# Two pools of weight buffers placed above the split activations in the on-chip memory

## The chip, the cores and the metric

The kernel runs on one core of one Trainium2 chip. The metric is the device time of one execution in microseconds (us), as the median of several runs; lower is better. Before the change it is 3458.62 us (three runs, 3456.98 to 3459.93).

## The reference

The reference computes two transformer-like blocks in float32 over 1024 tokens of 1024 features. The first block mixes the tokens by a gated linear attention in two directions (four heads) that starts from a context of 256 tokens, and by a gated spatial mix; the second by a recurrence with a short convolution and by attention inside a window of 128 tokens. Each block ends with a gated feed-forward layer of 2816 hidden features. Between them lie norms over the features. What costs time are the products of the activations with the weight matrices:

```python
x = x + g1 * mix_l
x = x + g2 * _swiglu(_modulate(_rmsnorm(x, norm2_g[l]), sh2, sc2), w_ffn_in[l], w_ffn_out[l])
...
proj = xn @ w_in[l]
...
x = x + merged @ w_out[l]
gu = xn2 @ w_ffn_in[l]
x = x + (jax.nn.silu(ff_gate) * ff_up) @ w_ffn_out[l]
```

## The kernel before, in words

Activations lie with 128 features on the partitions and the tokens along the row, in tiles of 128 by 512. To reach float32 accuracy each operand of a large product is held as two parts in the matrix format float32r, a high part and a low part, and each product is three matmuls: high weights by high activations, high weights by low activations, low weights by high activations. In `gemm` (lines 158 to 167) and in `product` of `ffn_in` and `ffn_out` (lines 1051 to 1053 and 1264 to 1266) the weights are the stationary operand, loaded anew for each matmul, 128 columns at a time, and the activations stream past them, nearly always 512 columns. In `gemm_tok` (lines 169 to 177) it is the other way round: a block of 128 tokens of the activations is stationary and the weights stream, 256 columns.

Weights come from memory into `raw` (2 buffers of 4 KB in each partition), and are split by `unit` (lines 139 to 152): ScalarE writes the high part `wh`, GpSimd (POOL) the low part `wl`, both in the pool `wp` (4 buffers of 4 KB of each name). The two feed-forward layers split quarters and sums of weights straight into `wp` by `split` (lines 190 to 193). SyncE issues the loads in the order of the program. Tiles that hold split activations for long come from the pool `hp` (32 buffers `hl` of 2 KB); others come from the pools of a phase, `slot` or `half`, which lie behind all of these. In the last of five blocks of each second feed-forward product the weights are kept: `supply` (lines 1202 to 1214) hands `unit` two buffers `hl` in which to put the two parts, so that the stationary operand comes from `hp` there and the streaming one from `half`. It does so in pieces of 512 columns in the first layer, and in pieces of 512 and 256 columns in the second.

The pools that live for the whole program are opened in `__init__` (lines 59 to 69), and each pool lies in a partition right behind the one opened before it. Their sizes follow from their tiles, in bytes of a partition: `raw` 8,192; `wp` 32,768; `tmp` (4 tiles `t` of 2 KB) 8,192; `sm` (small tiles: five names of 4 by 32 bytes, one of 4 by 64, five single ones of 64) 1,216; `hp` 65,536. In the compiled program of before `raw` starts at byte 20,992, which is 164 times 128, so `wp` starts at 29,184, `tmp` at 61,952, `sm` at 70,144, and `hp` at 71,360; the pools of the phases start at 136,896.

No order is written out by hand around the change: it touches no instruction, and every loop, queue and buffer count stays.

Of the kernel before, what the change touches and what calls it, by code (L numbers as in the profile page):

```python
# [16 lines left out]
P = 128  # L17
T = 1024
# [31 lines left out]
def hs(q):  # L50
    """The columns of half q of the tokens."""
    return slice(q * HQ, q * HQ + HQ)


class Prog:
    """Activations lie feature-major, [features on partitions, tokens], in tiles of 128
    features by 512 tokens; operands of the large products as exact sums of two float32r parts."""

    def __init__(self, tc, ins, out, ctx):
        self.tc, self.nc, self.I, self.out = tc, tc.nc, ins, out  # L60
        self.cst = self.pool(ctx, "cst", 1)
        self.raw = self.pool(ctx, "raw", 2)
        self.wp = self.pool(ctx, "wp", 4)
        self.tmp = self.pool(ctx, "tmp", 4)
        self.sm = self.pool(ctx, "sm", 4)
        self.hp = self.pool(ctx, "hp", 32)
        self.dr = self.pool(ctx, "dr", 1, space=bass.MemoryType.DRAM)
        self.bg, self.lag, self.loads = deque(), deque(), 0

# [28 lines left out]
    def slot(self, *dims, dt=F32):  # L98
        """[P, 1024] of the phase's storage, or less of it in the shape dims."""
# [8 lines left out]
    def half(self, dt=F32):  # L108
        """[P, 512] of the phase's storage."""
        return self.gp.tile([P, HQ], dt, name="half")  # L110
# [4 lines left out]
    def hnew(self, n=8):  # L115
        """A split activation, hi and lo, each n tiles of features by halves of tokens."""
# [22 lines left out]
    def unit(self, src, kt=8, width=P, eng=None, raw=None, into=None):  # L139
        """Load one block of weights (if it isn't in raw yet) and split it exactly into two float32r parts."""  # L140
# [13 lines left out]
    def wide(self, src, eng=None, raws=(None, None)):  # L154
        """Two blocks, 1024 x 256 together."""
        return [self.unit(src[i], kt=4, width=256, eng=eng if i else None, raw=raws[i]) for i in range(2)]

    def gemm(self, o, w, h, l, q, kt=8, s=slice(None), mid=None):
        """o[feature, token] = W^T X with both operands split; mid comes half way."""
# [9 lines left out]
    def gemm_tok(self, o, ws, h, l, t):  # L169
        """o[token, feature] = X W for the 128 tokens of block t."""  # L170
# [8 lines left out]
    def proj(self, src, fn, mid=None):  # L179
        """The products of one block of weights with both halves of the tokens."""  # L180
# [15 lines left out]
    def tick(self, n=1):  # L196
        """The next step of what runs beside the large products."""
# [14 lines left out]
    def store(self, dst, src):  # L212
        """A store that later loads need not wait behind."""
# [7 lines left out]
    def step(self, chunks, n=1):  # L221
        """One product after the other, with n steps of what runs beside them after each."""
# [5 lines left out]
    def square_into(self, acc, src, first, scale=1.0, eng=None):  # L228
        """acc += (scale * src)^2"""
# [6 lines left out]
    def squares(self, acc, src, eng):  # L236
        """The sum of the squares of tiles."""
# [4 lines left out]
    def token_sums(self, accs, ps, o):  # L242
        """ps[:, o + b] = sums over features for the tokens of block b."""
# [6 lines left out]
    def rsqrt(self, x):  # L250
        """1/sqrt of a small positive tile, by Newton's steps from the exponent's half."""
# [12 lines left out]
    def spread(self, r):  # L264
        """r holds a value for each token, tokens on partitions in blocks: the same on all
        partitions, tokens along the free axis."""
# [6 lines left out]
    def rstd(self, accs, n=D):  # L273
        """1/sqrt(mean of the squares + eps) in a bank, from sums of squares, in two steps."""
# [10 lines left out]
    def now(self, steps):  # L285
        """All steps at once."""
# [6 lines left out]
    def modulated(self, x, rs, A, B, hi, lo, eng=None):  # L293
        """hi + lo = x * A * rs + B"""
# [10 lines left out]
    def norm(self, q, acc, A, B=None):  # L305
        """Steps to the modulated norm of half q of self.x, in the form that ffn_in takes: with quarters Bij
        (i: half of the features, j: of the tokens), B11, B21, B22 and the sums T1..T4, all split."""
# [54 lines left out]
    def ada_first(self):  # L362
        """Shift and scale of the first norm, for the latents and the context, one half of the features after
        the other, by products; most of the scale by sums of weighted rows over k first. In steps."""
# [45 lines left out]
    def ada_one(self, m):  # L410
        """A block of gate 1, shift 2, scale 2, gate 2 of the latents; its sums over k and those of the
        block before over the partitions."""
# [19 lines left out]
    def ada_last(self):  # L432
# [5 lines left out]
        # the branches are summed twice as large  # L438
# [3 lines left out]
    def start(self):  # L442
# [5 lines left out]
        # resets of the scans at the chunks' first tokens  # L448
# [56 lines left out]
    def start_latents(self):  # L505
        """Steps to the norm of the latents."""
# [15 lines left out]
    def decays(self, st, n, zs, d):  # L522
        """Cumulated log decays (times GATE_TEMP) of direction d within each chunk, in steps.
        st: stacked low-rank inputs [96, n]; gives tiles that hold [P, NH, n] in order."""
# [29 lines left out]
    def low_rank(self, waf, st, h, l, n, q):  # L554
        """Inputs of the decays, stacked [hi; lo; hi]."""
# [23 lines left out]
    def latent_decays(self, stl, zs):  # L579
        """Decays of the latents, kept outside."""  # L580
# [36 lines left out]
    def context_states(self, st, zs):  # L617
        """Steps to the states that the context leaves, for both directions."""
        nc = self.nc
        self.Si = self.slots_of(2, NH, 256)  # L620
        for d in QS:
# [7 lines left out]
            # the half that is passed first decays through the other one too  # L629
# [17 lines left out]
    def ends(self, c, d):  # L647
        """Of chunked log decays: the chunks' totals, their exponentials, those of pairs."""
# [1218 lines left out]
```

## Time and profile before

| what | value |
|---|---|
| median of three runs | 3458.62 us (3456.98 to 3459.93) |
| span of the profiled execution, first to last instruction | 3453.9 us |
| what lies around the span, by the runs shown | 3.1 to 6.0 us |
| TensorE matmul busy | 3305.8 us, 96% |
| TensorE weight load busy | 2683.4 us, 78% |
| VectorE (DVE), ScalarE (ACT), GpSimd (POOL) busy | 61%, 39%, 45% |
| DMA | 97 GB/s over the span |

The profiled execution has no time of its own beside its span; the runs' times are a few microseconds longer, since they hold what comes before the first and after the last instruction. Matmuls run through a pipeline: the recorded duration of one (some 390 ns for 512 columns) is longer than the distance between the starts of two that follow each other, and that distance is what a stream of them costs.

### The profile page before, as it was taken

The page shows a single profiled execution, that of the slowest core. Times are in us where ns is not written, and L with a number is a line of the kernel's source. Part 1 is how long each engine was busy: PE and PEld are TensorE (multiplying, and loading weights), DVE is VectorE, ACT ScalarE, POOL GpSimd, SP SyncE. Part 2 cuts the span into 40 slices and gives each one's busy share as a digit, 9 for nine tenths or more (in the row PEclk, how much of TensorE's full clock was granted, in tenths as well). Part 3 has the DMA queues.
Part 4 walks back from the last instruction along what each step waited for, and adds up shares of the span by engine and source line. Part 5 has one row for each costly group of instructions (what it writes and reads, how often), then busy time and mean ns, then how long its engine had stood idle before and what let it go on. Part 6 is the DMA issues. An engine that isn't in the chain of part 4 may idle for free. (4 is left out here: it accounts for less than half of the span.)

```text
span 3453.9 us, 43238 instructions
## 1 busy us (share of the span) xinstructions
PE 3305.8 (96%) x15868; PEld 2683.4 (78%) x15868; DVE 2118.4 (61%) x3438; ACT 1364.3 (39%) x2396; POOL 1544.3 (45%) x991
## 2 busy tenths in 40 slices
PE   7999999999999999999999989999999999999997
PEld 4778888888888778888767867777777778887766
DVE  7554234333667385555698587777776585554786
ACT  4552222211122442232424486666665332232433
POOL 3222233222322675444656434444444775444764
PEclk9999999999999999999999999999999999999999
DMA  6121111244236522221352311111114432222342
GB/s 254 62 110 53 49 68 65 74 159 129 84 119 204 169 92 80 74 82 67 113 177 83 130 33 54 45 54 45 54 48 154 144 103 99 74 80 89 95 137 78
DMA packets 153012, 335.11 MB, mean 97 GB/s; under 512 B 20864, under 2 KB 29184, under 8 KB 152800
## 3 DMA queue, kind: packets, MB, share of 16 engines
q1 hardware_dynamic: 140640, 311.36, 26.8%
q10 hardware_dynamic: 12160, 20.98, 1.6%
q8 instruction: 126, 2.06, 0.2%
q14 instruction: 86, 0.70, 0.1%
HBM read 263.07 MB, written 69.21 MB: 96 GB/s over the span
## 5 line engine op out<-in xcount | busy, mean ns | idle before, releaser
L151 POOL TENSOR_TENSOR wl<-raw,wh 128x1024 fp32r<-128x1024 f32 (+1 forms) x188 | 426.7, 2273 | 751.2 <-ACT wh L150 629.9
L163 PE MATMUL mm<-hl,wh 128*128 128x512 f32 (+1 forms) x1584 | 643.3, 406 | 1.4 <-ACT t L1547 1.4
L165 PE MATMUL mm<-hl,wl 128*128 128x512 f32 (+1 forms) x1584 | 630.7, 398 | 1.6 <-POOL wl L151 1.6
L164 PE MATMUL mm<-hl,wh 128*128 128x512 f32 (+1 forms) x1584 | 631.7, 399 | 0.0
L193 POOL TENSOR_TENSOR wl<-half,wh 128x512 fp32r<-128x512 f32 x308 | 433.0, 1430 | 367.5 <-ACT wh L192 367.5
L150 ACT CAST wh<-raw 128x1024 fp32r<-128x1024 f32 (+3 forms) x189 | 177.4, 940 | 492.3 <-PE mm L164 232.4
L165 PEld LDWEIGHTS mm<-hl,wl 128*128 128x128 f32 (+1 forms) x1584 | 300.5, 190 | 74.6 <-POOL wl L151 2.4
L163 PEld LDWEIGHTS mm<-hl,wh 128*128 128x128 f32 (+1 forms) x1584 | 300.2, 190 | 66.6 <-ACT t L1547 1.8
L164 PEld LDWEIGHTS mm<-hl,wh 128*128 128x128 f32 (+1 forms) x1584 | 300.5, 190 | 64.9 <-issue 0.5
L192 ACT CAST wh<-half 128x512 fp32r<-128x512 f32 x308 | 178.6, 619 | 409.6 <-PE ax L1052 218.1
L1030 DVE TENSOR_TENSOR half<-half 128x512 f32<-128x512 f32 x176 | 202.1, 1188 | 3.0
L1606 POOL TENSOR_SCALAR p<-p,ast 128x384 f32<-128x384 f32 (+1 forms) x64 | 84.0, 1313 | 263.4 <-DVE ast L1604 162.5
L175 PE MATMUL mm<-wh,hl 128*128 128x256 f32 x576 | 163.5, 284 | 1.3 <-ACT wh L150 1.3
L177 PE MATMUL mm<-wl,hl 128*128 128x256 f32 x576 | 161.8, 281 | 1.9 <-POOL wl L151 1.9
L176 PE MATMUL mm<-wh,hl 128*128 128x256 f32 x576 | 162.2, 282 | 0.7 <-DVE hl L193 0.5
L1052 PE MATMUL mm<-hl,wh 128*128 128x512 f32 x360 | 142.8, 397 | 3.3 <-POOL hl L193 3.3
L1051 PE MATMUL mm<-hl,wh 128*128 128x512 f32 x360 | 142.6, 396 | 0.6 <-ACT hl L192 0.6
L1053 PE MATMUL mm<-hl,wl 128*128 128x512 f32 x360 | 142.4, 395 | 0.0
L1051 PE MATMUL ax<-hl,wh 128*128 128x512 f32 x344 | 136.5, 397 | 0.8 <-ACT hl L192 0.7
L1053 PE MATMUL ax<-hl,wl 128*128 128x512 f32 x344 | 136.2, 396 | 0.0
L1052 PE MATMUL ax<-hl,wh 128*128 128x512 f32 x344 | 136.0, 395 | 0.0
L193 POOL TENSOR_TENSOR wl<-raw,wh 128x384 fp32r<-128x384 f32 x96 | 113.8, 1204 | 37.1 <-ACT wh L192 37.1
(419 smaller groups left out, 7991.7 us busy)
## 6 DMA issues: line engine op xcount, KB each, us to landing
half<-in_w_fi SPq DMA_DIRECT2D x196, 256.0 KB, 4.7
hid<-t SPq DMA_DIRECT2D x78, 256.0 KB, 2.0
half<-hid SPq DMA_DIRECT2D x72, 256.0 KB, 4.5
raw<-in_w_ada SPq DMA_DIRECT2D x32, 512.0 KB, 3.7
raw<-in_w_o SPq DMA_DIRECT2D x32, 512.0 KB, 3.9
raw<-in_w_fo SPq DMA_DIRECT2D x32, 384.0 KB, 3.2
slot<-in_w_ada SPq DMA_DIRECT2D x16, 512.0 KB, 10.2
raw<-in_w_u SPq DMA_DIRECT2D x16, 512.0 KB, 3.6
```

The costliest lines, as they stand in the source:

```text
L150: nc.scalar.copy(hi, r)
L151: self.last_split = (eng or nc.gpsimd).tensor_tensor(lo, r, hi.bitcast(F32), op=ALU.subtract).ins
L163: mm(o, wh[:, k], h[k][q][:, s], start=k == 0, stop=False)
L164: mm(o, wh[:, k], l[k][q][:, s], start=False, stop=False)
L165: mm(o, wl[:, k], h[k][q][:, s], start=False, stop=k == kt - 1)
L175: mm(o, h[k][q][:, s], wh[:, k % 4], start=k == 0, stop=False)
L192: self.nc.scalar.copy(hi, x)
L193: (eng or self.nc.vector).tensor_tensor(lo, x, hi.bitcast(F32), op=ALU.subtract)
L1030: V.tensor_tensor(s, a, b, op=op)
L1051: mm(o, wh[:, k], h, start=k == 0, stop=False)
L1052: mm(o, wh[:, k], l, start=False, stop=False)
L1053: mm(o, wl[:, k], h, start=False, stop=k == 3)
```

## The change

The pools `raw` and `wp` are opened after `hp`, no longer before `tmp`. The remainder of the diff empties comments and docstrings, line for line, so that line numbers stay.

```diff
         self.cst = self.pool(ctx, "cst", 1)
-        self.raw = self.pool(ctx, "raw", 2)
-        self.wp = self.pool(ctx, "wp", 4)
         self.tmp = self.pool(ctx, "tmp", 4)
         self.sm = self.pool(ctx, "sm", 4)
         self.hp = self.pool(ctx, "hp", 32)
+        self.raw = self.pool(ctx, "raw", 2)
+        self.wp = self.pool(ctx, "wp", 4)
         self.dr = self.pool(ctx, "dr", 1, space=bass.MemoryType.DRAM)
```

## Rows read from the trace of the kernel before

**Rows 1.** The page: busy us, share of the span and instructions of each engine.
```profile
PE 3305.8 (96%) x15868; PEld 2683.4 (78%) x15868; DVE 2118.4 (61%) x3438; ACT 1364.3 (39%) x2396; POOL 1544.3 (45%) x991
```

**Rows 2.** Waits of PE, longest first: us in total, times, longest.
```profile
PE po L1630 <- DVE pt L193: 20.0, 7, 5.2
PE sc L1595 <- DVE pt L193: 11.0, 12, 1.7
```

**Rows 3.** Busy us (x instructions) of PE, PEld, DVE, ACT, POOL; clock, DMA share, GB/s.
```profile
1650.00:1850.00 200.00, 183.79 (x747) 142.34 (x746) 170.29 (x213) 77.42 (x152) 126.88 (x96) 0.97 0.41 133
1950.00:2650.00 700.00, 654.22 (x3109) 527.45 (x3109) 520.14 (x1057) 467.64 (x890) 289.41 (x161) 0.98 0.17 55
```

**Rows 4.** Timeline of PE, 2900 to 2945: start, duration; first and last of 194 matmuls.
```profile
2899.78 0.39 PE L1051 MATMUL mm<-hl,wh 128*128 128x512 f32 x1
...
2944.81 0.40 PE L1052 MATMUL mm<-hl,wh 128*128 128x512 f32 x1
```

**Rows 5.** Timeline of PE, 1861 to 1886.2: first and last of 113 matmuls.
```profile
1860.62 0.39 PE L164 MATMUL mm<-half,hl 128*128 128x512 f32 x1
...
1886.00 0.39 PE L165 MATMUL ax<-half,hl 128*128 128x512 f32 x1
```

**Rows 6.** The columns of rows 3, for three short stretches.
```profile
1861.00:1886.00 25.00, 25.00 (x112) 20.68 (x111) 16.11 (x24) 14.90 (x24) 7.24 (x6) 1.00 0.26 82
2900.00:2945.00 45.00, 45.00 (x194) 36.28 (x193) 27.28 (x31) 12.18 (x23) 21.99 (x16) 1.00 0.20 71
720.00:760.00 40.00, 40.00 (x176) 32.20 (x175) 9.71 (x24) 2.59 (x3) 4.78 (x2) 1.00 0.39 131
```

**Rows 7.** Timeline of PE, 725 to 743.5: first and last of 81 matmuls.
```profile
724.79 0.39 PE L164 MATMUL mm<-slot,wh 128*128 128x512 f32 x1
...
743.46 0.39 PE L163 MATMUL mm<-slot,wh 128*128 128x512 f32 x1
```

**Rows 8.** Matmuls of line 163: count, duration min/median/max in ns, first and last start.
```profile
L163 PE MATMUL mm<-hl,wh x1584: 387/394/799, 100.9 to 2736.3; 128*128 128x512 f32 x196, 128*96 128x512 f32 x2
...
L163 PE MATMUL mm<-slot,wh x168: 276/394/482, 40.6 to 812.0; 128*128 128x512 f32 x128, 128*128 128x256 f32 x32, 128*96 128x256 f32 x8
...
L163 PE MATMUL ax<-half,hl x80: 283/389/389, 1861.7 to 3438.4; 128*128 128x512 f32 x48, 128*128 128x256 f32 x32
```

**Rows 9.** PE and PEld of one line, whole span: lines 163, 1051, 1264, 175, in this order.
```profile
0.00:3454.00 3454.00, 915.54 (x2296) 434.45 (x2296) 0.99 0.29 97
...
0.00:3454.00 3454.00, 487.84 (x1232) 231.61 (x1232) 0.99 0.29 97
...
0.00:3454.00 3454.00, 137.25 (x336) 65.08 (x336) 0.99 0.29 97
...
0.00:3454.00 3454.00, 183.27 (x640) 123.41 (x640) 0.99 0.29 97
```

**Rows 10.** Timeline of PE, 301 to 306: first and last of 45 matmuls.
```profile
300.90 0.28 PE L177 MATMUL mm<-wl,hl 128*128 128x256 f32 x1
...
306.08 0.28 PE L176 MATMUL mm<-wh,hl 128*128 128x256 f32 x1
```

**Rows 11.** Timeline of PE, 3416.6 to 3418.9: first and last of 22 matmuls.
```profile
3416.33 0.28 PE L164 MATMUL ax<-half,hl 128*128 128x256 f32 x1
...
3418.85 0.28 PE L164 MATMUL mm<-half,hl 128*128 128x256 f32 x1
```

**Rows 12.** PE and PEld of line 163 alone, 1950 to 2650.
```profile
1950.00:2650.00 700.00, 296.28 (x717) 137.47 (x718) 0.98 0.17 55
```

**Rows 13.** Low parts split on POOL by line 193: count, duration min/median/max in ns.
```profile
L193 POOL TENSOR_TENSOR wl<-half,wh x308: 1277/1304/1847, 1193.3 to 3158.6; 128x512 fp32r<-128x512 f32 x154
...
L193 POOL TENSOR_TENSOR half<-half x32: 1276/1592/1840, 1240.2 to 3364.4; 128x512 fp32r<-128x512 f32 x32
```

**Rows 14.** DMA issues: KB each, median us from issue to landing.
```profile
raw<-in_w_u SPq DMA_DIRECT2D x16, 512.0 KB, 3.6
...
slot<-decay SPq DMA_DIRECT2D x8, 512.0 KB, 4.5
```

## The prediction, made before the changed kernel was run

> **What bounds the kernel now.** I read the page first: matmuls keep TensorE (PE) busy for 3305.8 of 3453.9 us, 96%; no other engine is above 61% [rows 1]. The list of PE's waits says the same: the two longest are 20.0 and 11.0 us in total, both behind VectorE in the windowed attention [rows 2]. By stretch, the mixers of the second block leave PE idle for 45.8 of 700 us and the second product of the first feed-forward layer for 16.2 of 200 [rows 3]; in the first product of such a layer it is busy for 45.00 of 45 us [rows 6]. So a change of where buffers lie can matter in two ways: through a transfer or a split that PE waits for, or through what a matmul itself costs.
>
> For the second I read timelines, since the recorded duration of a matmul overlaps its neighbours. In the feed-forward stretch at 2900 us, 194 matmuls of 512 columns without a wait start over 2899.78 to 2944.81: 45.03 / 193 = 233.3 ns each [rows 4]. At 1861 us, 113 of the same shape start over 1860.62 to 1886.00: 25.38 / 112 = 226.6 ns [rows 5]. The granted clock is 1.00, the 2.4 GHz level, in both [rows 6]. What differs is where the stationary operand lies: in `wh` and `wl` in the first, in `hl` in the second, the kept weights of the last block. Is it the work beside them? VectorE, ScalarE and POOL are busy for 64, 60 and 29% of the fast stretch and for 61, 27 and 49% of the slow one, and between 720 and 760 us for 24, 6 and 12% [rows 6], where weights from `wh` and `wl` still cost 233.4 ns (81 matmuls, 724.79 to 743.46, 18.67 / 80) [rows 7]. Whether `hl`, `half` or `slot` streams makes no difference either [rows 4, 7]. That leaves the address of the weights.
>
> **What the change does to addresses.** By the sizes given above, `tmp`, `sm` and `hp` move down by 8,192 + 32,768 = 40,960 bytes, a multiple of 128; `raw` and `wp` move up by 8,192 + 1,216 + 65,536 = 74,944, which is 585 times 128 plus 64. I call an address modulo 128 its phase. Before, `wp` is at phase 0 (29,184), `hp` at 64 (71,360), and so are `half` and `slot`, which don't move. After, `wp` starts at 104,128: phase 64, the same as everything that streams past it. The fast products of rows 5 have stationary and streaming operand both at phase 64; the slow ones of rows 4 and 7 have 0 and 64. Modulo 512 the new `wp` and the `hl` of rows 5 agree too (both 192). And `wp` comes to lie above 64 KB, as the `hl` of rows 5 does; by that account it would gain as well.
>
> **The terms.** No instruction, wait, buffer count or queue order changes, so nothing is moved past a queue.
>
> 1. *Products with weights from `wp`, 512 columns.* Line 163 runs 2296 times; 2 times 80 of these have weights in `hl` and 40 have 256 columns (of the 168 with `slot`), which leaves 2096; line 1051 runs 1232 times, line 1264 336 times [rows 8, 9]. Each has two sister lines: 3 x 3664 = 10,992 matmuls. At 233.3 - 226.6 = 6.7 ns each: **-73.6 us** of PE time.
>
> 2. *`gemm_tok`*: 3 x 640 = 1920 matmuls [rows 9], weights streaming in 256 columns past `hl` or `slot`. Now (phases 0 and 64) they cost 5.18 / 44 = 117.7 ns [rows 10]. With both at 64, the nearest row is the last block's pieces of 256 columns: 2.52 / 21 = 120.0 ns [rows 11]. **+4.4 us.** Bounds: nothing, and the 4.4. The 120 matmuls of 256 columns past `slot` weights at the start: the same 2.3 ns, +0.3.
>
> 3. *What waits take back.* In the mixers 717 x 3 of these products run [rows 12], worth 14.4 us; beside them VectorE is busy for 520 of 700 us and PE idles 45.8 [rows 3]. A product that ends sooner there partly waits longer for the softmax. Between losing none and all I take half, 7.2, because PE is busy far longer than it waits, but the attention's chain is not shortened. The Strassen blocks of the two second feed-forward products (336 x 3 products, 6.8 us) and their plain blocks run beside similar waits [rows 3]; with the plain blocks (some 4 us) I take a third of 10 us, 3.4.
>
> 4. *Splits.* ScalarE, POOL and VectorE now read and write `raw`, `wh`, `wl` at another phase. POOL's shortest split into `wl` (phase 0) is 1277 ns, into `half` (phase 64) 1276 [rows 13]: nothing, either way.
>
> 5. *Loads.* Rows of `raw` began at a multiple of 256 bytes and will begin 192 past one. A `raw` load lands in 3.6 us; `slot`, which begins 192 past one, takes 4.5 for the same 512 KB [rows 14], though from another source. So 0 to 0.9 us more per load. Cover: the weights are prefetched over four buffers and PE's longest waits are for none of them [rows 2]. I take 0, and 5 us for the top of the range.
>
> Sum: -73.6 + 4.4 + 0.3 + 7.2 + 3.4 = -58.3 us, **-58** rounded. Against the profiled execution: 3453.9 - 58.3 = 3395.6 us of span; the median of the runs stands 4.7 us above the span of before, so the median becomes 3458.6 - 58.3 = **3400 us**. Differences under 0.2% (7 us) can't be told from no change here.
>
> **The rivals.** *No change, 3459 us.* The 6.7 ns have another cause (the order of the buffers, the shorter kept blocks), or the pools end at other phases than I worked out. For it: the fast rows come from one kind of block alone. Against it: 113 matmuls in one stretch keep 226.6 ns whatever runs beside. The Trainium skill speaks for this rival: "TensorE: Matmul & The Clock Gate", Part 2, gives PE two independent read ports and says that loading the next weights doesn't steal bandwidth from the running matmul; by it an address could not matter, and the time would stay 3459. The measured 233.3 and 226.6 ns at one clock disagree with it. Chance 0.09.
>
> *Part of it, 3444 us.* The fast rows have `half` streaming, never `hl`. If an `hl` that streams doesn't gain, 7632 of the 10,992 matmuls drop out (line 163 x1584 [rows 8], and about six tenths of lines 1051 and 1264), leaving 3360 x 6.7 = 22.5, less 4.7 and some 3 for waits: -15 us. Against it: in the slow rows `hl`, `half` and `slot` cost the same. Chance 0.06.
>
> *Slower, 3537 us.* With 256 columns both operands at phase 64 are the dearer case, 120.0 against 117.7 ns [rows 10, 11]. If a 512-column product of `wp` followed that (2 x 120.0 = 240.0 ns), each would lose 6.7 ns, +73.7 and the +4.7 of term 2. It decides where the distance of two starts passes 233.3 ns. Against it: the 512-column rows themselves, at 226.6. Chance 0.04.
>
> **How the numbers follow.** The main case has 0.81 and gives 3400 us. Its range: if waits take nothing back and `gemm_tok` stays, 3458.6 - 73.6 = 3385, 2 us lower for what rounding leaves; if the mixers and the second feed-forward products lose all (14.4 + 10) and the loads cost 5, 3458.6 - 73.6 + 4.7 + 24.4 + 5 = 3419, 1 more for rounding. So 3383 to 3420, with 0.19 outside. Faster by over 0.2%: main case and the partial one, 0.87; within 0.2%: 0.09; slower: 0.04.
>
> **What would show it.** In the profile after: 233.3 becomes 226.6 ns in the stretch of the first feed-forward product, whatever streams; the recorded 394 ns of products with `wh` falls to the 389 of those with `hl` [rows 8]; `gemm_tok` goes to 120.0; the feed-forward stretches shorten by nearly 3% (6.7 of 233.3), the mixers by about half of 14 us, PE's waits for VectorE there grow; the last block is unchanged. I am wrong if the distance stays at 233.3, if only products with `half` change, or if PE's waits for `wh` and `wl` grow.

## The result, and the profile after

The changed kernel takes **3422.84 us** (median of 4 runs, 3418.96 to 3423.99) against 3457.95 us for the kernel before, in the same comparison: a ratio of **0.9897** (95% interval 0.9883 to 0.9911), 35.1 us less. The forecast was 3400 us, 3383 to 3420: right in sign and in what changes the price of a product, 23 us too low, and just outside its range. The profiled executions differ by 31.6 us (spans of 3453.9 and 3422.3 us). In the runs that give both, the time is some 1.8 us longer than the span (3423.99 us for the span of 3422.3), so the profiled execution of before took about 3455.7 us and not its median: it was some 2 us faster than the median, the one of after 1 us slower, and that is the rest of the 35.1. (The 4.7 us by which the prediction set the median above the span hold both.)

From the page of the changed kernel, part 1 (busy time, share, instructions), answering to [rows 1]:

```profile
PE 3259.1 (95%) x15868; PEld 2693.3 (79%) x15868; DVE 2120.3 (62%) x3438; ACT 1362.6 (40%) x2396; POOL 1537.2 (45%) x991
```

PE is busy for 46.7 us less with the same 15,868 matmuls; the other engines differ by 7 us at most, so the splits cost about what they cost before. 46.7 us of recorded work went, 31.6 us of span: PE idles 15 us longer.

First what a matmul costs now. The timeline of PE in the feed-forward stretch (start, duration), first and last of 174 matmuls without a wait, answering to [rows 4]:

```profile
2865.74 0.39 PE L1051 MATMUL ax<-half,wh 128*128 128x512 f32 x1
...
2904.95 0.39 PE L1053 MATMUL ax<-half,wl 128*128 128x512 f32 x1
```

39.21 / 173 = 226.6 ns, where it was 233.3. The same view around 303 us, second and last of 45 matmuls of `gemm_tok`, answering to [rows 10]:

```profile
300.88 0.28 PE L176 MATMUL mm<-wh,hl 128*128 128x256 f32 x1
...
306.04 0.28 PE L177 MATMUL mm<-wl,hl 128*128 128x256 f32 x1
```

5.16 / 43 = 120.0 ns, up from 117.7, as forecast. The list of line 163's matmuls (count, duration min/median/max in ns), answering to [rows 8]:

```profile
L163 PE MATMUL mm<-hl,wh x1584: 387/389/796, 101.2 to 2714.1; 128*128 128x512 f32 x196, 128*96 128x512 f32 x2
...
L163 PE MATMUL mm<-slot,wh x168: 276/389/476, 40.8 to 805.0; 128*128 128x512 f32 x128, 128*128 128x256 f32 x32, 128*96 128x256 f32 x8
...
L163 PE MATMUL mm<-half,hl x80: 278/389/499, 1838.8 to 3405.6; 128*128 128x512 f32 x48, 128*128 128x256 f32 x32
```

The recorded 394 ns of products with `wh` are the 389 of those with `hl`, whatever streams.

So in this stretch the price of a product came out to the tenth of a nanosecond, and the time did not. Where it went is seen by stage. Both kernels issue the same instructions in the same order on every engine, so each matmul of one trace has its partner in the other; the table holds how much later (+) or earlier (-) a stage's matmuls end against their partners than they began, beside what terms 1 and 2 of the prediction make of the products that lie in it (us of the kernel before):

```
stage                                from   to   terms 1, 2  measured  taken back
first block, heads                      0   790     -10.3      -6.4       3.9
start of the spatial branch           790   900      +1.0      +4.2       3.2
spatial branch, first merge           900  1200      -7.4      -7.3       0.1
ffn 1, first product                 1200  1650     -12.6     -11.0       1.6
ffn 1, second product, keys/values   1650  1950      -5.3      +0.9       6.2
mixers of the second block           1950  2650     -14.4      -1.5      12.9
second merge                         2650  2770      -3.3      -1.0       2.3
ffn 2, first product                 2770  3195     -11.9     -11.6       0.3
ffn 2, second product                3195  3400      -4.9      +0.9       5.8
last norm                            3400  3454       0.0      +1.2       1.2
sum                                                 -69.1     -31.6      37.5
```

An entry of one pair of profiles is good to some 2.5 us: the kernel before and `diff128` (below), both at 233 ns, differ by up to 2.6 us in a stage of the same table. In the first products of the feed-forward layers and in the spatial branch the changed kernel kept nearly everything. In the mixers and in the two second products of the feed-forward layers it kept next to nothing. The windows of those stretches in the changed kernel (busy us (x instructions) of PE, PEld, DVE, ACT, POOL; clock, DMA share, GB/s), answering to [rows 3]:

```profile
1630.00:1830.00 200.00, 180.25 (x744) 140.48 (x743) 168.20 (x210) 77.39 (x152) 123.14 (x95) 0.97 0.41 132
1930.00:2629.00 699.00, 649.17 (x3111) 529.59 (x3110) 519.12 (x1057) 468.11 (x891) 288.99 (x161) 0.97 0.17 56
```

PE idles for 19.8 of 200 us, where it was 16.2, and for 49.8 of 699, where it was 45.8: as long a stretch with less work in it. PE's waits in the whole span of the changed kernel, answering to [rows 2] (us in total, times, longest):

```profile
PE po L1630 <- DVE pt L193: 20.1, 7, 5.3
PE sc L1595 <- DVE pt L193: 11.8, 13, 1.9
PE po L1630 <- DVE slot L1635: 8.9, 8, 1.2
```

All three belong to the attention; the first two were 20.0 and 11.0 us [rows 2]. In the mixers of the kernel before, the third of them and the one that grew most read

```profile
PE po L1630 <- DVE slot L1635: 8.3, 8, 1.2
PE po L1630 <- ACT pt L192: 2.0, 6, 0.3
```

and that last one in the mixers of the changed kernel

```profile
PE po L1630 <- ACT pt L192: 4.5, 8, 0.7
```

The same waits, each a little longer.

They are not the whole of it. Taken distance by distance (from one start to the next, against its partner in the other trace), about 15.6 of the 37.5 us lie where PE waits in one of the two traces, 9.4 where the granted clock is at its 1.2 GHz level in one of them, and 12.3 in series of matmuls at full clock without a wait. In those series the products with weights from `wp` became 5.7 ns cheaper on the mean, not 6.7, and in the mixers only 4.2: from 233.4 to 229.2 ns. The timeline of PE shows it behind six matmuls of the attention: the first, seventh and eleventh product in the changed kernel, then the first and twelfth of their partners before:

```profile
2105.47 0.39 PE L163 MATMUL mm<-hl,wh 128*128 128x512 f32 x1
2106.85 0.39 PE L163 MATMUL mm<-hl,wh 128*128 128x512 f32 x1
2107.76 0.39 PE L164 MATMUL mm<-hl,wh 128*128 128x512 f32 x1
```

```profile
2126.30 0.39 PE L163 MATMUL mm<-hl,wh 128*128 128x512 f32 x1
2128.87 0.40 PE L165 MATMUL mm<-hl,wl 128*128 128x512 f32 x1
```

Before, the distances are 233 or 234 ns from the first on. In the changed kernel the first six are 229 to 236 ns and only the next four 226 or 227. Over all such series in the mixers, the first two distances are 232 to 234 ns on the mean in both kernels; from the twentieth on they are 233.5 before and 227.2 in the changed kernel. `low64` and `all0` (below) show the same, with means of 228.9 and 229.4 ns in the mixers. Why the first products behind others do not get cheaper is open.

### The profile page after: what moved, and what is told of

Its sections match the earlier page's. It is cut to its first block, busy times and chain, and to the rows that moved or that the text cites. A ratio compares the mean times of both kernels' runs of the same rounds, so it can differ in the third digit from the quotient of the medians.

```text
span 3422.3 us, 43238 instructions
## 1 busy us (share of the span) xinstructions
PE 3259.1 (95%) x15868; PEld 2693.3 (79%) x15868; DVE 2120.3 (62%) x3438; ACT 1362.6 (40%) x2396; POOL 1537.2 (45%) x991
## 5 line engine op out<-in xcount | busy, mean ns | idle before, releaser
L163 PE MATMUL mm<-hl,wh 128*128 128x512 f32 (+1 forms) x1584 | 636.1, 402 | 1.7 <-ACT t L1547 1.4
L164 PE MATMUL mm<-hl,wh 128*128 128x512 f32 (+1 forms) x1584 | 623.4, 394 | 0.0
```

Of the source, the lines that this page charges most:

```text
L163: mm(o, wh[:, k], h[k][q][:, s], start=k == 0, stop=False)
L164: mm(o, wh[:, k], l[k][q][:, s], start=False, stop=False)
```

## The experiments

### Where, or at which phase?

The change moves the pools above 64 KB and alters their phase (address modulo 128) at once. Four kernels take the two apart, with nothing but padding.

`low64`: the order of before, `wp` low, but at phase 64:

```
         self.cst = self.pool(ctx, "cst", 1)
+        self.pool(ctx, "pad0", 1).tile([P, 16], F32, name="pad0")
         self.raw = self.pool(ctx, "raw", 2)
         self.wp = self.pool(ctx, "wp", 4)
+        self.pool(ctx, "pad1", 1).tile([P, 16], F32, name="pad1")
         self.tmp = self.pool(ctx, "tmp", 4)
```

> Order of the pools as before (raw and wp below 64 KB, below hp), but 64 bytes of padding ahead of raw and 64 more ahead of tmp: wh and wl lie at 29,248 to 62,016, phase 64, while tmp stays at phase 0 and hl, half and slot stay at phase 64. Theory A (the address modulo 128 of the stationary operand against that of the streaming one decides): the products of 512 columns start every 227 ns as in the changed kernel, gemm_tok every 120 ns, and the time is that of the changed kernel, 3423 us (3415 to 3430). Theory B (where the pools lie decides, above or below 64 KB or next to hp): the products stay at 233 ns and the time at 3458 us. Theory C (the order in which the pools stand and the distance of hl from wp): 3458 us too.

`high0`: the order of the change, with the same two pads around `raw` and `wp`, which puts `wp` at phase 0 above 64 KB.

> Order of the pools as in the changed kernel (raw and wp above hp and above 64 KB), with 64 bytes of padding ahead of raw and 64 behind wp: wh and wl lie at 104,192 to 136,960, phase 0, and hl, half and slot at phase 64 as in both kernels. Theory A (phase): the products of 512 columns cost 233 ns, gemm_tok 118 ns, and the time is that of before, 3458 us (3450 to 3465). Theory B (the place above 64 KB): 227 ns and 3423 us.

`all0`: the order of before with one pad ahead of `hp`; everything at phase 0.

> Order of the pools as before, with 64 bytes of padding ahead of hp alone: raw, wp, hl, half and slot all lie at phase 0. Theory A1 (equal phase is all that counts): 227 ns for 512 columns, 120 ns for 256, and about 3423 us. Theory A2 (each line of 128 bytes that the streaming operand touches costs 13.3 ns; 512 columns of 4 bytes touch 17 lines at phase 64 and 16 at phase 0, 256 columns 9 and 8): 213.3 ns for 512 columns and 106.7 ns for 256, 20.0 and 11 ns less than before; 10,992 and 1,920 of them are 220 and 21 us of TensorE's time, and if waits take back four tenths of that, as they did in the changed kernel beyond its mixers, or less, the time is 3230 to 3320 us.

`s0w64`: `low64` with a third pad ahead of `hp`; weights at phase 64, what streams at 0.

> Order of the pools as before, with 64 bytes of padding ahead of raw, of tmp and of hp: wh and wl at phase 64, and hl, half and slot at phase 0, so unequal again but with the streaming operand at 0. Theory A1 (equal phase counts): as before, 233 ns and 3458 us. Theory A2 (lines of 128 bytes that the streaming operand touches, and 6.7 ns more where the phases differ): 213.3 + 6.7 = 220.0 ns for 512 columns; gemm_tok, whose streaming operand is wh and wl at phase 64, stays at 118 to 120 ns; the time then lies between that of all0 and that of the changed kernel.

Measured: `low64` 3420.09 us (ratio 0.9893, 0.9878 to 0.9908), `high0` 3446.31 (0.9972, 0.9961 to 0.9984), `all0` 3422.36 (0.9897, 0.9882 to 0.9911), `s0w64` 3426.72 (0.9915, 0.9898 to 0.9931). For the price of a product one window does, 2800 to 3100 us, where PE never waits: 300 us over the count of matmuls (first column after the times). In this order the kernel before, the changed kernel, `low64`, `high0`, `all0`, `s0w64`, each a row of its own trace:

```profile
2800.00:3100.00 300.00, 300.00 (x1288) 241.70 (x1287) 177.32 (x212) 84.30 (x148) 153.37 (x111) 1.00 0.27 91
```

```profile
2800.00:3100.00 300.00, 300.00 (x1325) 248.50 (x1324) 177.14 (x209) 87.72 (x156) 154.63 (x113) 1.00 0.24 85
```

```profile
2800.00:3100.00 300.00, 300.00 (x1325) 248.42 (x1324) 177.08 (x210) 87.71 (x155) 153.59 (x112) 1.00 0.25 84
```

```profile
2800.00:3100.00 300.00, 300.00 (x1299) 243.78 (x1298) 178.26 (x211) 87.53 (x154) 154.32 (x111) 1.00 0.26 89
```

```profile
2800.00:3100.00 300.00, 300.00 (x1325) 248.43 (x1324) 177.07 (x210) 87.75 (x155) 154.10 (x113) 1.00 0.25 84
```

```profile
2800.00:3100.00 300.00, 300.00 (x1312) 246.14 (x1312) 177.68 (x208) 86.69 (x155) 153.44 (x111) 1.00 0.25 85
```

1325 matmuls (226.4 ns) wherever the pools lie, if weights and streaming operand agree, be it at 64 or at 0: the place above 64 KB has no part in it (theory B falls, and C with it), and neither has the number of 128-byte lines (theory A2 falls with `all0`). But phase modulo 128 is not the whole rule either. `high0` and `s0w64`, with unequal phases, came in at 230.9 and 228.7 ns, between the two values, and `high0` 4 us under its expected range. Sorted by what streams, `high0` has 233.2 ns past `hl` and 229.6 past `half` and `slot` (means over the starts without a wait). Its `wp` lies, modulo 256, 64 above `hl` and 192 above `half`; in `s0w64` all differences are 192, and in the kernel before 64.

### The price by itself

`scan` leaves the reference out altogether and issues groups of 24 matmuls, moving each operand on its own:

```
for ox in range(0, 64, 8):
    for ow in range(0, 64, 8):
        group(ow, ox, 512, 24)   # matmul(ps, w[:, o + ow:o + ow + P], x[:, ox:ox + cols]), o = 128 * (i % 8)
```

> No part of the reference is computed: the kernel is a row of matmuls alone, in float32r, each with a weight load of its own, 24 in a group, with stationary and streaming operand moved in steps of 32 bytes over 256 (64 groups of 512 columns, 64 of 256), and four groups with the weights moved by 4, 8, 16 and 48 bytes. Theory A1' (from the runs so far: the distance of two starts goes by the stationary operand's address less the streaming one's, modulo 256): 544 cycles, 226.7 ns, at 0; about 560 cycles, 233.3 ns, at 64; about 550, 229.5 ns, at 192, whatever the two addresses are by themselves; other differences lie between 226 and 234 ns or, at 128, at 226.7 again. Theory A2' (it goes by each address by itself): the distances differ along a line of equal difference. If any difference costs less than 226 ns, a kernel with it would beat both kernels.

The timeline of PE inside one group each, 21 matmuls (start, us from the first start to the last end): streaming operand at offset 0 and weights at 0, 64, 128, 192 bytes; then streaming at 64 and weights at 64, 128, 192.

```profile
20.60 4.93 PE L1793 MATMUL ps<-x,w 128*128 128x512 f32 x21
31.66 5.06 PE L1793 MATMUL ps<-x,w 128*128 128x512 f32 x21
42.87 5.06 PE L1793 MATMUL ps<-x,w 128*128 128x512 f32 x21
54.07 4.97 PE L1793 MATMUL ps<-x,w 128*128 128x512 f32 x21
120.84 4.93 PE L1793 MATMUL ps<-x,w 128*128 128x512 f32 x21
131.90 5.06 PE L1793 MATMUL ps<-x,w 128*128 128x512 f32 x21
143.11 5.06 PE L1793 MATMUL ps<-x,w 128*128 128x512 f32 x21
```

Less the last one's 0.39 us and over 20 distances: 227.0 ns at difference 0, 233.5 at 64 and at 128, 229.0 at 192. The last three repeat the first three, since only the difference counts. Over all 64 groups of 512 columns, in cycles of 2.4 GHz from the mean of the last 19 distances of a group: 544 to 545 (226.7 ns) at difference 0, 549 to 550 (229 ns) at 192, and 558 to 562 (233 to 234 ns) at 32, 64, 96, 128, 160 and 224; at differences of 4, 8, 16 and 48 bytes 558, 553, 560 and 560. Equal addresses modulo 256 are the cheapest of all that were tried and the only ones at 226.7 ns. With 256 columns equal addresses cost 287 to 288 cycles, a difference of 160 as much, and the others 272 to 288: the case in which equality costs.

The Trainium skill's "TensorE: Matmul & The Clock Gate", Part 2, gives PE two independent read ports, one for what streams and one for the weights. These rows differ: with little else running, the address of the one against that of the other moves the distance by 3%.

### The prediction's own rule, put to the test

The prediction had said "modulo 128". `diff128` keeps the changed kernel's phases and moves `wp` by 128 bytes against all the others:

```
         self.hp = self.pool(ctx, "hp", 32)
+        self.pool(ctx, "pad0", 1).tile([P, 32], F32, name="pad0")
         self.raw = self.pool(ctx, "raw", 2)
         self.wp = self.pool(ctx, "wp", 4)
+        self.pool(ctx, "pad1", 1).tile([P, 32], F32, name="pad1")
```

> The changed kernel with 128 bytes of padding ahead of raw and 128 behind wp: wh and wl at 104,256, still phase 64 modulo 128 like hl, half and slot, but 128 away from them modulo 256. By the rule of the prediction (equal address modulo 128) the time is that of the changed kernel, 3423 us, at 227 ns a product. By the row of matmuls alone (equal modulo 256; 560.5 cycles at a difference of 128) the products cost 233.5 ns and the time is 3450 to 3462 us.

Measured: 3454.68 us (ratio 0.9998, 0.9988 to 1.0007), and in the window

```profile
2800.00:3100.00 300.00, 300.00 (x1287) 241.34 (x1287) 176.69 (x211) 86.88 (x153) 151.14 (x110) 1.00 0.26 89
```

233.1 ns: the whole gain is gone, 128 bytes from where it was. The rule is modulo 256.

### Who takes the gain back in the mixers?

`noatt_before` and `noatt_after` leave out the attention's steps, with 128 bytes of padding ahead of `hp`:

```
-                self.bg.append(self.attention(j, K, F[j]))
+                F[j]["o"] = self.slot()
+                self.nc.gpsimd.memset(F[j]["o"], 0.0)
```

> The kernel before without the attention's steps in the mixers of the second block (scores, softmax, transposes, values; the output of that branch is set to zero instead, queries and keys are still made). 128 bytes of padding ahead of hp keep every address modulo 256 as before. A base for its partner: the mixers then take less than 600 us, and their products of 512 columns start every 233.3 ns.

> The changed kernel without the attention's steps, in the same way. Theory M (the chain of the attention through VectorE and ScalarE sets the end of each of the eight tiles, so that what TensorE gains there is waited away): without it, the mixers are 10 to 14.4 us shorter than in its partner of before, where the whole kernels differ there by 1.5. Rival (the gain is lost to something else, such as a lower granted clock or dearer steps on the other engines): 1 to 4 us.

3286.62 and 3242.72 us in one run each: 43.9 us apart, where the whole kernels are 35. The mixers, between the same two matmuls, in the one and in the other:

```profile
1950.00:2490.00 540.00, 534.57 (x2257) 421.51 (x2255) 300.97 (x241) 303.50 (x379) 217.88 (x109) 0.99 0.25 77
```

```profile
1932.17:2461.65 529.48, 520.93 (x2257) 422.33 (x2255) 304.39 (x240) 304.19 (x379) 217.77 (x109) 0.99 0.25 78
```

540.0 against 529.5: 10.5 us of the 14.4 come through, not 1.5, as Theory M expected: the attention is what takes the gain back. How it does so is shown only in part, since the edit takes away its matmuls on PE, its work on VectorE and ScalarE and the waits for them at once. Waiting the gain away for the chain, as Theory M has it, is the smaller part: of the 12.9 us of the mixers 4.0 lie in waits, 3.1 at the low level of the clock and 5.8 in series without a wait (in `low64` 5.0, 0.2 and 5.5). Without the attention the distances in such series go from 233.3 to 227.2 ns. (One profile of a stretch differs from another by some us: with the attention, the mixers of the kernels at 226.7 ns, the changed one, `low64` and `all0`, take 698.7, 696.4 and 695.7 us, those of the kernels at 233.3 ns 700.1 and 697.5. That is 2 us on the mean.)

### Who takes it back in the second feed-forward products?

From the last product of lines 1051 to 1053 to the first one with kept weights, both layers together, the kernel before takes 211.8 + 208.3 = 420.2 us, the changed one 212.4 + 209.4 = 421.7, `low64` 419.3, `all0` 418.5, `diff128` 418.5: no difference at all between 226.7 and 233.3 ns.

VectorE was the first suspect: in the changed kernel it is busy for 168 of 200 us there. `relief_before` and `relief_after` take the sums of line 1282 to POOL and the terms of line 1519 to ScalarE:

```
-                    V.tensor_tensor(was[0], was[0], was[1], op=add)
+                    nc.gpsimd.tensor_tensor(was[0], was[0], was[1], op=add)
...
-            nc.vector.scalar_tensor_tensor(t, dist, -2.0 ** (-0.5 * (i + 1)), mk, op0=ALU.mult, op1=ALU.add)
+            nc.scalar.activation(t, dist, AF.Copy, scale=-2.0 ** (-0.5 * (i + 1)))
```

> The kernel before, with two kinds of work taken off VectorE in the second products of the feed-forward layers: the 16 sums of line 1282 (936 ns each, in both layers) go to POOL, and the 16 terms of line 1519 (675 ns each, in the first layer only) to ScalarE; the results are the same up to the masked terms. Theory V (VectorE, 91 to 95% busy from 1700 to 1850 us, sets the pace of these blocks): the stretch of the first such product gets 5 to 10 us shorter, that of the second 2 to 5, and the time is 3443 to 3451 us. Theory W (the splits of the weights on POOL set it): POOL gets 22 us more in each product, and the time stays at 3456 us or rises by up to 10.

> The same two edits on the changed kernel. Theory V: besides what the edits bring in the kernel before, the gain of the addresses comes through in these two products, 3.9 and 3.6 us of shorter distances each where the changed kernel shows a gain of 0 or less: the two stretches together are 5 to 9 us shorter than in the relieved kernel before, and the time is 3402 to 3412 us. Theory W: 3423 us or more, and the two stretches no shorter than in the relieved kernel before.

3470.48 us (ratio 1.0037, 1.0020 to 1.0055) and 3431.99 (0.9927, 0.9905 to 0.9949): the first is slower than without, the second by its median, though its interval meets the changed kernel's. The two stretches take 429.1 and 427.5 us. Theory V falls, W is nearer: in the second layer's stretch of `relief_before`, PE now waits for the weights that POOL splits,

```profile
PE mm L1266 <- POOL wl L193: 5.8, 5, 1.5
```

where the kernel before waits 1.6 us for them.

The second suspect were the two buffers of `raw`. `raws_before` and `raws_after` load every other group of a Strassen block's weights elsewhere:

```
+                    if p % 2:
+                        (a11, a12), (a21, a22) = [[self.half()[:, :w] for _ in QS] for _ in QS]
+                        for i, pair in enumerate(((a11, a12), (a21, a22))):
+                            for c, r in enumerate(pair):
+                                nc.sync.dma_start(r, wo[2 * p + i][:, f0 * P + c * w:f0 * P + (c + 1) * w])
+                    else:
...
```

> The kernel before; in the Strassen blocks of the second feed-forward products every other group of weights (four of each block) is loaded into four buffers of half instead of the two of raw, by four transfers of 192 KB instead of two of 384. Theory R (in these blocks the two raw buffers turn once in 15.2 us, load and splits one after the other, while the group's 63 products need 14.7, and this cycle sets the pace): the loads no longer wait for the splits before them, and the two stretches get 4 to 15 us shorter together: 3443 to 3454 us. Rival P (POOL's splits and sums set it by themselves) and rival Q (the queue of SP, on which the loads stand behind others): within 3 us of before, or slower.

> The same edit on the changed kernel. Theory R: the cycle out of the way, the 6.3 ns a product come through in these blocks as well: the two stretches are 4 to 7 us shorter than in the edited kernel before, where without the edit the changed kernel gains nothing in them (+0.7 and +1.0 us); the time is 3403 to 3415 us, under both kernels. Rivals P and Q: 3420 to 3427 us.

3461.16 us (1.0014, 1.0004 to 1.0023) and 3423.42 (0.9907, 0.9892 to 0.9922): nothing won. The two stretches take 420.3 and 418.7 us, 1.6 apart where Theory R asked for 4 to 7. In the second Strassen blocks waits did go (the 50 us from 3290 on shrink to 47), but in the first one a new one appears, behind VectorE:

```profile
PE mm L1270 <- DVE t L1327: 5.6, 1, 5.6
```

as VectorE's timeline shows there, where it idles 4.80 us for a group's weights with the sum that PE waits for next in its queue:

```profile
1741.56 0.67 DVE L1243 TENSOR_TENSOR t<-half 128x384 f32<-128x384 f32 x1 [4.80 <-DMA half<-in_w_fo]
1742.16 0.68 DVE L1327 TENSOR_TENSOR t<-t,mm 128x512 f32<-128x512 f32 x1
```

(lines from 1228 on are 6 further down in these kernels). So the edit was turned round: groups 0 and 2 instead of 1 and 3 go to `half`, and the terms of line 1519 are made by ScalarE, as in `relief_before`, and stored by it too (`ev_before`, `ev_after`), or all four groups go to `half` besides (`allh_after`, with `if True` in the first line). Against `raws_before` and `raws_after`:

```
-                    if p % 2:
+                    if p % 2 == 0:
...
-            nc.sync.dma_start(self.abias[i // 2][:, i % 2], t)
+            nc.scalar.dma_start(self.abias[i // 2][:, i % 2], t)
```

> The same two edits on the kernel before. Theory R2: 3435 to 3450 us, and 4 to 7 us more in the two stretches than in the edited changed kernel, since the gain of the addresses comes through there once these waits are gone. Rival: 3453 to 3462 us, and no difference in the two stretches beyond the 1 to 2 us by which profiles of one stretch differ.

> The changed kernel; in the Strassen blocks the groups 0 and 2 of weights (no longer 1 and 3) are loaded into buffers of half, so that a block's first group need not wait for the splits of the plain block ahead of it; and the terms of line 1519 are made and stored by ScalarE, so that neither VectorE nor SP's queue has anything to do with them. Theory R2 (the loads of the weights, each waiting for the splits of the one before, and VectorE standing behind them, hold TensorE at the start of the blocks and of each group; every such wait ends at a time that TensorE's speed has no part in): the waits at the two starts of Strassen blocks (some 8 us lost at each, half of it at the low level of the clock) shrink to less than half, the two stretches of 200 us get 8 to 25 us shorter, and the time is 3398 to 3415 us. Rival (other waits of the same size stand right behind): 3418 to 3428 us.

> As the edited changed kernel, but all four groups of each Strassen block go into buffers of half, so that the two raw buffers serve the plain blocks alone and the plain blocks' first weights need not wait either. Theory R2: 2 to 6 us less again than with every other group. Against it: 44 buffers of half may not hold four more groups, and loads then wait for those; the time then rises above that of the kernel with every other group.

`ev_before` 3449.14 us (0.9974, 0.9963 to 0.9985), `ev_after` 3416.97 (0.9879, 0.9864 to 0.9894), `allh_after` **3411.62** (0.9867, 0.9851 to 0.9884). The last is 47.0 us under the kernel before of its comparison, where the changed kernel was 35.1 under; the intervals of the two ratios only touch. In its windows of the two stretches

```profile
1626.40:1833.38 206.98, 190.12 (x795) 152.26 (x793) 167.71 (x208) 88.50 (x174) 133.55 (x100) 0.96 0.43 136
3138.57:3335.35 196.78, 186.11 (x795) 149.61 (x793) 151.18 (x189) 78.22 (x157) 146.26 (x112) 0.98 0.39 125
```

the two take 403.8 us together instead of 421.7. But the gain of the addresses still doesn't come through: `ev_before` 410.5 us, `ev_after` 409.3. Theory R2 is right that the loads cost time here: from `ev_after` to `allh_after`, where the loads alone differ, the two stretches get 5.5 us shorter (what `ev_before` wins comes of the loads and of line 1519 together). It is wrong that they alone hide PE's gain.

The last pair takes the Strassen blocks away:

```
-FF_BLOCKS = (("P", 3), ("W", 6), ("P", 3), ("W", 6), ("P", 4))
+FF_BLOCKS = (("P", 3),) * 6 + (("P", 4),)
```

> The kernel before with the hidden features of the second feed-forward products in seven plain blocks (six of 3 tiles, one of 4) instead of plain and Strassen blocks in turn: 36 products of 512 columns more for each Strassen block that goes, but none of its sums, splits of sums and gathers on VectorE, POOL and ScalarE. A base for its partner: the six blocks take 864 products at 233.3 ns, 202 us, and waits.

> The same on the changed kernel. Theory E (in the Strassen blocks the other engines' work sets when a product can start, so that the 6.7 ns are waited away; in plain blocks TensorE sets the pace): the six blocks are 4.5 to 5.8 us shorter than in the partner of before in each of the two layers (864 times 6.7 ns is 5.8), where the kernels with Strassen blocks differ by +0.7 and +1.0 us. Rival (the gain is lost in these stretches whatever the other engines do, for instance through the transfers or the clock): within 2 us of each other.

3460.12 and 3423.56 us in one run each. The two stretches in `plain_before`, then in `plain_after`:

```profile
1641.81:1857.37 215.56, 206.42 (x867) 164.45 (x866) 101.71 (x136) 60.73 (x110) 82.19 (x72) 0.98 0.42 134
3174.31:3392.78 218.47, 207.91 (x866) 164.56 (x865) 89.85 (x118) 59.14 (x109) 80.74 (x71) 0.98 0.37 117
```

```profile
1624.58:1836.34 211.76, 202.14 (x867) 164.18 (x865) 100.94 (x136) 60.41 (x110) 83.69 (x72) 0.98 0.43 136
3140.95:3356.75 215.80, 204.39 (x866) 165.64 (x865) 90.11 (x118) 59.33 (x109) 80.59 (x71) 0.97 0.37 119
```

The first of these stretches in the changed kernel, with its Strassen blocks, reads

```profile
1626.46:1838.83 212.37, 192.16 (x795) 150.01 (x793) 179.03 (x225) 80.87 (x159) 130.00 (x100) 0.97 0.41 133
```

VectorE falls from 179 to 101 us, POOL from 130 to 84, and the gain appears: 3.8 and 2.7 us. That is less than the 4.5 expected at least, and more than the rival's 2, though one profile of a stretch differs from another by as much as the margin. What is lacking lies in waits (0.9 us in each stretch) and at the low level of the clock (1.0 and 1.9); after the first 50 us the gain is the full 2.9% (0.72 us in each 25). So the runs point to the work of the Strassen blocks beside the matmuls, on several engines at once, as what holds PE there. Which of it comes last at each place is not settled: relieving one engine won nothing, and loading the weights earlier won the same in both kernels.

## Why the prediction was wrong

- **Term 2 was right, and term 1 in its price and its cause, not in its count.** In the feed-forward stretch a product of 512 columns costs 226.6 ns, and one of 256 columns 120.0, wherever the pools lie. Of the three rivals, "no change" and "slower" fall with the first rows above, "part of it" with line 163's 389 ns for products with `hl` streaming. But term 1 took 6.7 ns off each of the 10,992 products, and in the mixers, where short series of them stand between the attention's matmuls, they became 4.2 ns cheaper.
- **The reason given for term 1 was too coarse.** The rows of before held no pair of operands 128 bytes apart modulo 256, so "modulo 128" and "modulo 256" could not be told apart; the change moves `wp` against `hl` by 74,944 + 40,960 = 115,904 bytes, which turns a difference of 64 modulo 256 into 0. Had it been 128 more, the rule as stated would have forecast 3400 and the result would have been 3455, as `diff128` shows. That it came out rests on a remark beside the rule, that the new `wp` agrees with the `hl` of rows 5 modulo 512 too; the forecast made no condition of it.
- **Terms 4 and 5 were right as far as they went.** The other engines' busy times hardly move, and the page gives the loads of `w_u` into `raw` 3.7 us to landing where it gave 3.6 [rows 14], the others of that size between 0.1 less and 0.3 more. But a load that takes as long as before can be a longer wait for a faster PE: at the start of the spatial branch PE's wait for `wh`, which ScalarE makes from a load of `raw`, grew from 1.3 to

```profile
PE mm L175 <- ACT wh L150: 3.4, 1, 3.4
```

  It is 2.2 and 3.0 us in `low64` and `all0`, at 226.7 ns a product, and 1.0 in `diff128`, at 233.

- **Term 3 is the step that failed: "what waits take back", put at 7.2 + 3.4 = 10.6 us; 37.5 were taken back** (by the medians 69.1 - 35.1 = 34.0). Of these, the mixers took 12.9 (half of 14.4 was assumed, nearly all of it went) and the second feed-forward products with keys and values 12.0 (a third of 10 was assumed; all of it went, and 2 more). The other 12.6 us lie where the prediction assumed nothing: at the start of the spatial branch, in the second merge and among the heads. The reason given for the half, that PE is busy far longer than it waits, does not carry: the mixers, in which PE is busy for 93%, gave back nine tenths. Nor is it the waits alone. They took 15.6, half as much again as the term; the 9.4 at the low level of the clock and the 12.3 of products that became cheaper by less than 6.7 ns had no term at all. Which of the attention's parts keeps those products dear stays open.
- **The clock took a part of it.** The timeline of PE in the changed kernel, first feed-forward layer:

```profile
1754.45 0.39 PE L164 MATMUL mm<-half,wh 128*128 128x512 f32 x1
1757.00 0.50 PE L165 MATMUL mm<-half,wl 128*128 128x512 f32 x1 [2.15 <-POOL wl L151]
...
1758.42 0.63 PE L164 MATMUL mm<-half,wh 128*128 128x512 f32 x1
1758.85 0.63 PE L165 MATMUL mm<-half,wl 128*128 128x512 f32 x1
...
1760.98 0.62 PE L164 MATMUL ax<-half,wh 128*128 128x512 f32 x1
```

  After a start 2.55 us behind the one before it and a few at or near the usual distance, eight matmuls start 0.43 us apart instead of 0.23, which is the 1.2 GHz level; the window from 1757.50 to 1761.00 has a granted clock of 0.58. In the kernel before, the same start was 2.16 us behind, and none of those that follow it is slow. The longer wait does not decide it by itself: in `low64`, `all0` and `s0w64` the same start is 2.49, 2.50 and 2.57 us behind, and none that follows is slow. So what such a stretch costs differs from one execution to the next. Products of 512 columns whose next start is 0.40 to 0.46 us away number 138 in the trace of before and 160 in that of after (124 in `diff128`, 147 and 161 in `low64` and `all0`): 22 times 0.2 us are some 4 of the 37.5, about half of what lies at the low level. Of the 1.2 us that the last norm lost, nearly all is of this kind; in the window from 3387 to 3407 us

```profile
3387.00:3407.00 20.00, 18.27 (x140) 18.07 (x140) 15.98 (x32) 9.28 (x22) 11.93 (x12) 0.91 0.31 113
```

  the granted clock is 0.91, and 1.00 in its partner of before. `low64`, with 1.00 there too, lost 0.3 us in the last norm.
- The chances (0.87 for faster) were sound. The range was too narrow at the top: its upper end let the mixers and the second feed-forward products lose all, but took nothing for the other stages, the clock, or products that gain less.

## What to carry to other kernels

When a change makes every instruction of the busiest engine a little cheaper, sum the gain stage by stage, and keep it only where that engine runs long rows of them without a wait for another one. In a stretch with other matmuls between them and pieces that end on another engine's chain, count on little of it, however busy the engine looks: here 1.5 to 4.4 of 14.4 us came through in the mixers (changed kernel, `low64`, `all0`). A rule on addresses that is read from two values holds for those two: put the shortest scan that moves one operand past the other ahead of the change itself. For float32r products of 512 columns here, that gives weights and streaming operand at the same address modulo 256.

## What the runs showed of the hardware that had not been expected

- With weights loaded for each matmul, the distance of two float32r matmuls of 512 columns goes by the difference of the operands' addresses modulo 256, in steps of 32 bytes: 226.7 ns at 0, 229 at 192, 233 to 234 at the six others; 4, 8 and 16 bytes off cost 232.5, 230.5 and 233.4. In the 64 pairs of `scan` the two addresses by themselves play no part. With 256 columns equality is among the dear cases: 119.8 ns at 0, 120.0 at 160, 117 to 119 at the others.
- In the mixers the first products behind other matmuls do not get the lower price: in the changed kernel 232 to 233 ns for the first two distances of a series, 227.2 from the twentieth on.
- 128 bytes of padding are worth 32 us of this kernel: `diff128` 3454.68 us, the changed kernel 3422.84.
- The same wait of PE (2.49 to 2.57 us from start to start) was followed by a stretch at the 1.2 GHz level in two traces (the changed kernel, `high0`) and by none in three; after 2.16 and 2.24 us (the kernel before, `diff128`) none followed.
